# RWKV recursion in a two-layer trunk: ties as quarter-array matmuls, keys by token through transposes, key planes by factor, a fixed chain order

## The chip, the cores and the metric

One core of one Trainium2 chip. The metric is the device time of one execution in microseconds (us); the median of three runs is given, and one profiled execution beside it. PE is the matmul engine (TensorE), PEld its weight loads, DVE VectorE, ACT ScalarE, POOL GpSimd, SP the engine that issues DMAs.

## The reference

A decoder trunk of two layers on x of 1 x 512 x 1024, all in float32: a SwiGLU half, attention, a SwiGLU half; then a SwiGLU half, RWKV-7 time mixing, a SwiGLU half. The change lies in the time mixing alone, 16 heads of 64, whose core is a recursion over the tokens:

```python
def rwkv7_step(state, inp):
    r_t, w_t, k_t, v_t, a_t, b_t = inp
    sa = jnp.einsum('bhvk,bhk->bhv', state, a_t)
    state = (state * w_t[:, :, None, :] + sa[..., None] * b_t[:, :, None, :]
             + v_t[..., None] * k_t[:, :, None, :])
    return state, jnp.einsum('bhvk,bhk->bhv', state, r_t)
...
    seqs = (tm(r_h), tm(w_h), tm(k_h), tm(v_h), tm(-kk), tm(kk * a_h))
    _, y = lax.scan(rwkv7_step, jnp.zeros((B, H, N, N), f32), seqs)
```

## The kernel before

The recursion is done in 8 chunks c of 64 tokens (C = 64, NC = 8), for two groups sg of eight heads. A group is four pairs j (m = 4 sg + j), the two heads of a pair on partitions 0 to 63 and 64 to 127. Within a chunk the tokens are tied to each other through a triangular system; between chunks a state of 64 x 64 per head is handed on.

- rw_prep (L1211, per pair) makes the planes of a pair. From the projected k and the gates it forms the scaled queries ar (plane 0 for the a factor, plane 1 for r), the decay at each chunk's end pend, and the scaled keys bk: k x pi and a x pi (a holds the b factor by then), interleaved by head, tokens side by side. DVE writes the one that belongs to a head's own half (L1263), POOL the other (L1264). Matmuls of 64 x 64 (L1271, 16 per pair) tie keys to queries, DVE masks them into u (L1272), and SP writes u as 32 x 32 tiles to DRAM (L1285, four per pair). rw_prep_all runs the four pairs of a group step by step.
- rw_inverse (L1307) loads the tiles back (L1315), DVE eliminates in 62 small operations (L1324, L1328), ACT transposes (L1329), four small loads and matmuls (L1356, L1363) complete the 64 x 64 inverses.
- rw_prep2 (L1288) forms the r plane on POOL (L1296) and per-head sums (L1297 DVE, L1300 PE).
- rw_ties (L1367), per chunk: POOL makes a diagonal dp of pend (L1379); 8 matmuls (L1384) tie both scaled keys to both queries into two banks, one by head, with 64 rows of the array for each; DVE masks them into am (L1386); 4 matmuls (L1389) with bk against dp give the keys by token, scaled; ACT copies them to bs (L1390); SP fetches v (L1395).
- rw_recur (L1398), per chunk: the right side from v and state (L1417, L1421), an ACT copy (L1427), the solve with the inverse (L1431), ACT copies (L1433), the state update (L1438 on PE, L1441 POOL, L1442 or L1444 DVE), the ties of the next chunk, the output y (L1449, L1453), four ACT copies of y (L1457).
- rw_post and rw_out (L1461, L1498) normalise y, transpose v back (L1480) and project with wo. L1052 and L1021 are the gate's expansion and per-head sums of the same part; L286 to L288 are the three products of a split-float32 matmul.

Nothing here is a table of numbers: a planner in the tile framework sets each engine's order at build time from its own model of times (TileContext with schedule_with_timeline_sim), subject to data dependences and to `self.after(x, y)`, which only demands that x come later than y in the order. "bank(name, n)" takes one of n PSUM banks of that name in turn. The callers, in the order of the text:

```python
        self.rw_prep_all(0)
...
        self.rw_inverse(0, mid)
        self.rw_prep_all(1)
...
        self.rw_prep2(1)
        self.rw_inverse(1, None)
        self.rw_recur(0)
...
        self.rw_recur(1)
        z = self.rw_post(0)
```

An f32 matmul shows in the trace as two instructions (two loads, two matmuls), in the listings of the order as one row.

## Time and profile before

| | us |
|---|---|
| median of 3 runs | 2183.55 (2183.04 to 2183.78) |
| the profiled execution | 2181.74 |
| its span, first to last instruction | 2179.5 |
| mean granted PE clock | 0.984 |

The profile counts an engine as busy while an instruction of it runs. In tables by stretch, PEclk is the granted clock as a share of 2.4 GHz. In brackets behind a row stands the idle time ahead of it and what ended it. The time mixing spans about 1380 to 1800 us; the rest are the attention and the SwiGLU halves.

### The profile page before, as it was taken

What the parts mean: (1) busy time and instruction counts of PE and PEld (TensorE: products, weight loads), DVE (VectorE), ACT (ScalarE), POOL (GpSimd) and SP (SyncE); (2) the same over time, 40 slices, a digit from 0 to 9 for tenths busy, and PEclk for the clock granted to TensorE, in tenths of its full rate; (3) what the DMA queues carried; (4) which work ended last, traced back from release to release, by engine and by line L of the source; (5) the groups of instructions that cost most, each with busy time, mean ns of one, the idle gap of its engine ahead of it and who ended that gap; (6) DMA issues with size and microseconds to landing.
All of it is one profiled execution on the core that took longest, in us unless ns stands there. A gap on an engine that the chain in (4) does not pass through costs nothing.

```text
span 2179.5 us, 28535 instructions
## 1 busy us (share of the span) xinstructions
PE 2136.5 (98%) x11431; PEld 1729.6 (79%) x11431; DVE 1185.3 (54%) x1595; ACT 775.9 (36%) x1196; POOL 219.8 (10%) x224
## 2 busy tenths in 40 slices
PE   8999999999999999999999999999989999999999
PEld 6888887867988888888888888767658768888887
DVE  5444445377478554447545445668576555444443
ACT  4222224345326332335333333462513334222222
POOL 2000002010011000002000000153462101000000
PEclk9999999999999999999999999999979999999999
DMA  5232323411018555555555655457633143232331
GB/s 177 78 116 78 111 92 108 121 49 54 20 58 268 190 184 184 170 192 188 169 191 156 184 172 162 171 164 223 178 112 91 51 158 97 77 116 81 108 102 58
DMA packets 264092, 286.56 MB, mean 131 GB/s; under 512 B 45139, under 2 KB 221419, under 8 KB 263960
## 3 DMA queue, kind: packets, MB, share of 16 engines
q1 hardware_dynamic: 261848, 282.65, 41.7%
q10 hardware_dynamic: 2112, 2.10, 0.3%
q8 instruction: 89, 1.46, 0.3%
q14 instruction: 43, 0.35, 0.0%
HBM read 229.85 MB, written 56.68 MB: 131 GB/s over the span
## 4 chain that ended last, share of the span: by engine, by line
PE 90%; DVE 6%; DMA 1%; ACT 1%; issue 1%; SPq 0%; POOL 0%; DVEq 0%; ACTq 0%; POOLq 0%
PE b L286 22%; PE b L287 22%; PE b L288 22%; PE am L286 3%; PE am L287 3%; PE am L288 3%; DVE const L1324 1%; PE ra L1384 1%; PE rm L286 1%; PE rm L287 1%; PE rm L288 1%; PE wo L287 1%; PE wo L286 1%; PE wo L288 1%; DVE heads L1263 1%; PE rq L1021 1%
## 5 line engine op out<-in xcount | busy, mean ns | idle before, releaser
L287 PE MATMUL b<-xg,parts 128*128 128x512 f32 x1408 | 548.5, 390 | 0.0
L286 PE MATMUL b<-xg,parts 128*128 128x512 f32 x1408 | 547.1, 391 | 1.2 <-ACT xg L385 0.8
L288 PE MATMUL b<-xg,parts 128*128 128x512 f32 x1408 | 547.7, 390 | 0.0
L258 DVE TENSOR_TENSOR parts<-const,parts 128x1024 fp32r<-128x1024 f32 (+2 forms) x320 | 362.1, 1138 | 292.2 <-ACT parts L257 291.6
L257 ACT CAST parts<-const 128x1024 fp32r<-128x1024 f32 (+2 forms) x320 | 312.2, 976 | 476.9 <-PE b L287 398.4
L286 PEld LDWEIGHTS b<-xg,parts 128*128 128x128 f32 x1408 | 264.6, 188 | 57.7 <-ACT xg L385 1.2
L287 PEld LDWEIGHTS b<-xg,parts 128*128 128x128 f32 x1408 | 264.7, 188 | 56.2 <-issue 1.0
L288 PEld LDWEIGHTS b<-xg,parts 128*128 128x128 f32 x1408 | 264.4, 188 | 55.0 <-issue 0.2
L288 PE MATMUL b<-act,parts 128*128 128x512 f32 x704 | 273.3, 389 | 0.0
L287 PE MATMUL b<-act,parts 128*128 128x512 f32 x704 | 273.2, 389 | 0.0
L286 PE MATMUL b<-act,parts 128*128 128x512 f32 x704 | 272.4, 390 | 0.0
L373 POOL TENSOR_TENSOR ssum<-ssum,sq 128x512 f32<-128x512 f32 x42 | 66.0, 1571 | 1211.3 <-ACT sq L372 544.8
L288 PEld LDWEIGHTS b<-act,parts 128*128 128x128 f32 x704 | 132.2, 188 | 27.5
L286 PEld LDWEIGHTS b<-act,parts 128*128 128x128 f32 x704 | 132.2, 188 | 27.3
L287 PEld LDWEIGHTS b<-act,parts 128*128 128x128 f32 x704 | 132.2, 188 | 27.2
L498 DVE SCALAR_TENSOR_TENSOR const<-b,const 128x512 f32<-128x512 f32 x128 | 87.3, 687 | 113.2 <-PE b L288 113.2
L291 ACT CAST act<-u 128x512 fp32r<-128x512 f32 x88 | 54.6, 622 | 246.5 <-DVE u L484 246.5
L483 DVE TENSOR_TENSOR u<-b,rstd 128x512 f32<-128x512 f32 x88 | 60.5, 690 | 148.0 <-PE b L288 147.9
L92 ACT ACTIVATE g<-g 128x512 f32<-128x512 f32 x88 | 55.2, 630 | 190.3 <-DVE g L478 190.3
L478 DVE TENSOR_TENSOR g<-b,rstd 128x512 f32<-128x512 f32 x88 | 60.2, 688 | 95.5 <-PE b L288 95.3
L292 DVE TENSOR_TENSOR act<-u,act 128x512 fp32r<-128x512 f32 x88 | 60.5, 689 | 36.5 <-ACT act L291 36.2
L484 DVE TENSOR_TENSOR u<-u,g 128x512 f32<-128x512 f32 x88 | 60.5, 691 | 2.7
(329 smaller groups left out, 2692.3 us busy)
## 6 DMA issues: line engine op xcount, KB each, us to landing
const<-in_ffn_w_gate_dram SPq DMA_DIRECT2D x88, 512.0 KB
const<-in_ffn_w_up_dram SPq DMA_DIRECT2D x88, 512.0 KB
parts<-pparts SPq DMA_DIRECT2D x68, 512.0 KB
parts<-parts SPq DMA_DIRECT2D x68, 512.0 KB
const<-in_ffn_w_down_dram SPq DMA_DIRECT2D x64, 512.0 KB
const<-in_ffn_w_down_dram SPq DMA_DIRECT2D x48, 256.0 KB
const<-in_attn_w_in_dram SPq DMA_DIRECT2D x24, 512.0 KB
lora<-pparts SPq DMA_DIRECT2D x8, 576.0 KB
```

What stands on the lines that cost most here:

```text
L92: ins = nc.scalar.activation(out, in_, func, **kw)
L257: self.nc.scalar.copy(hi[:r, :n], raw[:, :n])
L258: self.lo_engine.tensor_tensor(out=lo[:r, :n], in0=raw[:, :n], in1=hi[:r, :n].bitcast(F32), op=ALU.subtract)
L286: self.after(mm(out, lhs[0], rhs[0], start=start, stop=False), self.gate)
L287: mm(out, lhs[0], rhs[1], start=False, stop=False)
L288: self.last_mm = mm(out, lhs[1], rhs[0], start=False, stop=stop)
L292: self.nc.vector.tensor_tensor(out=lo, in0=t, in1=hi.bitcast(F32), op=ALU.subtract)
L373: nc.gpsimd.tensor_tensor(out=ssum, in0=ssum, in1=sq, op=ALU.add)
L478: nc.vector.tensor_tensor(out=g, in0=ps[i], in1=rstd, op=ALU.mult)
L483: nc.vector.tensor_tensor(out=u, in0=ps[2 + i], in1=rstd, op=ALU.mult)
L484: nc.vector.tensor_tensor(out=u, in0=u, in1=gs[i], op=ALU.mult)
L498: nc.vector.scalar_tensor_tensor(out=self.x[c], in0=ps, scalar=0.5, in1=self.x[c], op0=ALU.mult, op1=ALU.add)
```

## The change

In rw_prep the interleaved bk goes; two planes take its place, kp (from k) and bp (from a), each written by one DVE product over all 128 partitions (L1260 and L1261 after). POOL has no product there any more. In rw_ties POOL multiplies the keys of the chunk by pend into dp (same size as the diagonal was). The ties become 16 matmuls of 64 rows by 64 columns, 128 moving columns each, in the order pair, factor, head, each chained behind the one before; the banks "ra" are three instead of two. The keys by token come from four PE transposes of dp and three ACT copies. In rw_recur the next chunk's L1422 (after) must come behind the solve of the chunk before, L1456 behind the state update, and y is copied by one ACT instruction. Line numbers after the change are a few lower in rw_prep (L1271 is L1268, L1272 is L1269, L1386 is L1388) and a few higher in rw_recur (L1421 is L1427, L1431 is L1437, L1438 is L1445).

```diff
--- before.py
+++ after.py
@@ -1256,23 +1256,20 @@
         )
         pend = self.pend[:, sg, j, :, None]
         nc.gpsimd.tensor_copy(pend, ar[:, 1, :, C - 1 : C])
-
-        bk = heads[:, 2:4].rearrange("p e c t -> p (e c t)").rearrange("p (c e t) -> p c e t", c=NC, e=2)
-        for hh in range(2):
-            hs = slice(hh * 64, (hh + 1) * 64)
-            nc.vector.tensor_tensor(out=bk[hs, :, hh, :], in0=ch(k)[hs], in1=ch(pi)[hs], op=ALU.mult)
-            nc.gpsimd.tensor_tensor(out=bk[hs, :, 1 - hh, :], in0=ch(a)[hs], in1=ch(pi)[hs], op=ALU.mult)
+        kp, bp = heads[:, 2], heads[:, 3]
+        nc.vector.tensor_tensor(out=kp, in0=ch(k), in1=ch(pi), op=ALU.mult)
+        nc.vector.tensor_tensor(out=bp, in0=ch(a), in1=ch(pi), op=ALU.mult)
         yield
 
         ps = self.bank("rq", 3).rearrange("p (c t) -> p c t", c=NC)
         for c in range(NC):
             for hh in range(2):
                 own, oth = self.halves[hh]
-                mm(ps[oth, c, :], bk[own, c, 1 - hh, :], ar[own, 0, c, :], start=True, stop=True)
+                mm(ps[oth, c, :], bp[own, c, :], ar[own, 0, c, :], start=True, stop=True)
         nc.vector.tensor_tensor(
             out=u, in0=ps, in1=self.cmask[:, 0:1, :].to_broadcast([P, NC, C]), op=ALU.mult
         )
-        rw[m] = dict(ar=ar, bk=bk, u=u)
+        rw[m] = dict(ar=ar, kb=(kp, bp), u=u)
 
         if j == 0:
             rw["lin", sg] = self.dram.tile([P, 1024], F32, name=f"lin{sg}")
@@ -1373,21 +1370,29 @@
         bn = bs[:, 0].rearrange("p (j h d) -> p j h d", j=4, h=2)
         sv = bs[:, 1].rearrange("p (h j d) -> p h j d", h=2, j=4)
 
-        dp = self.diag[:, c % 2].rearrange("p (j d) -> p j d", j=4)
-        pend = self.pend[:, sg, :, c, None].to_broadcast([P, 4, P])
-        ident = self.ident[:, None, :].to_broadcast([P, 4, P])
-        self.after(nc.gpsimd.tensor_tensor(out=dp, in0=ident, in1=pend, op=ALU.mult), self.go)
-        ps = [self.bank("ra", 2).rearrange("p (j n) -> p j n", j=4) for _ in range(2)]
+        kb = rw["heads", sg][:, :16].rearrange("p (j i) c t -> p j i c t", i=4)[:, :, 2:, c, :]
+        dp = self.diag[:, c % 2].rearrange("p (j e t) -> p j e t", j=4, e=2)
+        pend = self.pend[:, sg, :, c, None, None].to_broadcast([P, 4, 2, C])
+        self.after(nc.gpsimd.tensor_tensor(out=dp, in0=kb, in1=pend, op=ALU.mult), self.go)
+        ps, ins = [self.bank("ra", 3).rearrange("p (j n) -> p j n", j=4) for _ in range(2)], None
         for j in range(4):
             pp = rw[4 * sg + j]
-            for h, (own, _) in enumerate(self.halves):
-                mm(ps[h][:, j, :], pp["bk"][own, c], pp["ar"][own, :, c, :], start=True, stop=True)
+
+            for e in range(2):
+                for h in range(2):
+                    own, to = self.halves[h][0], self.halves[h][e]
+
+                    prev, ins = ins, mm(ps[h][to, j, :], pp["kb"][e][own, c, :], pp["ar"][own, :, c, :], start=True, stop=True)
+                    self.after(ins, prev)
         for h in range(2):
             nc.vector.tensor_tensor(out=am[:, h], in0=ps[h], in1=mask, op=ALU.mult)
-        ps = self.bank("ra", 2)
+        ps = self.bank("ra", 3)
         for j in range(4):
-            mm(ps[:, j * P : (j + 1) * P], rw[4 * sg + j]["bk"][:, c], dp[:, j, :], start=True, stop=True)
-        nc.scalar.copy(bs[:, 0], ps)
+            nc.tensor.transpose(ps[:, j * P : (j + 1) * P], self.diag[:, c % 2, j * P : (j + 1) * P], self.ident)
+        ps = ps.rearrange("p (j h d) -> p j h d", j=4, h=2)
+        nc.scalar.copy(bn[:, :, 0], ps[:, :, 0])
+        for own, oth in self.halves:
+            nc.scalar.copy(bn[own, :, 1], ps[oth, :, 1])
 
         b, r0 = c // 2, (c % 2) * 64
         src = rw["vcd"][b][r0 : r0 + 64, :].rearrange("p (m h d) -> p m h d", h=2, d=C)
@@ -1406,7 +1411,7 @@
         self.am = self.t("am", [2, 2, 4, 2 * C]) if sg else self.shaped(self.raw_all[:, :2048], [2, 2, 4, 2 * C])
         self.bs = self.t("bs", [2, 2, S]) if sg else self.shaped(self.call[:, N_CONST + 4 * S : N_CONST + 8 * S], [2, 2, S])
         self.go = self.rr[0, 3] if sg else self.mid
-        st = None
+        st = solved = None
         am, bn, sv = self.rw_ties(sg, 0)
         for c in range(NC):
             b1 = self.bank("rr", 3).rearrange("p (q j v) -> p q j v", q=2, j=4)
@@ -1414,7 +1419,8 @@
             ps = b1[:, 0]
             for j in range(4):
                 for h, (own, oth) in enumerate(self.halves):
-                    mm(ps[oth, j, :], am[own, h, j, :C], sv[own, h, j, :], start=j == 0, stop=c == 0 and j == 3)
+                    ins = mm(ps[oth, j, :], am[own, h, j, :C], sv[own, h, j, :], start=j == 0, stop=c == 0 and j == 3)
+                    self.after(ins, solved)
             if c:
                 for j in range(4):
                     for h, (own, oth) in enumerate(self.halves):
@@ -1428,14 +1434,15 @@
             ps = b2[:, 0]
             for j in range(4):
                 for h, (own, oth) in enumerate(self.halves):
-                    mm(ps[oth, j, :], pairs[j]["u"][oth, c, :], rhs[oth, j, :], start=True, stop=True)
+                    solved = mm(ps[oth, j, :], pairs[j]["u"][oth, c, :], rhs[oth, j, :], start=True, stop=True)
+            moved = solved
             for h, (own, oth) in enumerate(self.halves):
                 nc.scalar.copy(sv[oth, h], ps[oth])
             if c < NC - 1:
                 ps = b2[:, 1]
                 for j in range(4):
                     for h, (own, _) in enumerate(self.halves):
-                        mm(ps[own, j, :], bn[:, j, h, :], sv[:, h, j, :], start=True, stop=True)
+                        moved = mm(ps[own, j, :], bn[:, j, h, :], sv[:, h, j, :], start=True, stop=True)
                 if c:
                     pend = self.pend[:, sg, :, c, None].to_broadcast([P, 4, C])
                     nc.gpsimd.tensor_tensor(out=part, in0=st, in1=pend, op=ALU.mult)
@@ -1446,15 +1453,15 @@
             py = b1[:, 1]
             for j in range(4):
                 for h, (own, oth) in enumerate(self.halves):
-                    mm(py[own, j, :], sv[:, h, j, :], am[:, h, j, C:], start=j == 0, stop=c == 0 and j == 3)
+                    ins = mm(py[own, j, :], sv[:, h, j, :], am[:, h, j, C:], start=j == 0, stop=c == 0 and j == 3)
+                    self.after(ins, moved)
             if c:
                 for j in range(4):
                     for h, (own, oth) in enumerate(self.halves):
                         self.rr[sg, NC] = mm(
                             py[own, j, :], st[own, j, :], pairs[j]["ar"][own, 1, c, :], start=False, stop=j == 3
                         )
-            for j in range(4):
-                nc.scalar.copy(pairs[j]["ar"][:, 0, c, :], py[:, j, :])
+            nc.scalar.copy(self.rw["heads", sg][:, 0:16:4, c, :], py)
             if c < NC - 1:
                 st, am, bn, sv = new, am2, bn2, sv2
 
```

PE in the first prep, at the third and fourth pair's products of keys and queries. Before:

```order
L288 MATMUL rm<-parts,xm 128x512
L1271 MATMUL rq<-heads 64x64 x16
L1021 MATMUL rq<-norms,const 8x512
L1271 MATMUL rq<-heads 64x64 x15
L1021 MATMUL rq<-norms,const 8x512 x2
```

After, at the same place:

```order
L287 MATMUL rm<-parts,xm 128x512
L1268 MATMUL rq<-heads 64x64 x32
L1021 MATMUL rq<-norms,const 8x512 x3
L288 MATMUL rm<-parts,xm 128x512
L286 MATMUL rm<-parts,xm 128x512
```

Before, 17 more matmuls of L1271 stand ahead, with five projection products (L286 to L288) between them and the first row shown, so that the two pairs come in three pieces; after, both pairs are one block of 32 (L1268), with the three L1021 behind it.

DVE in the second prep, from the last two pairs' products to the last mask. Before:

```order
L1263 TENSOR_TENSOR heads<-kr,heads 64x8x64 x2
L1272 TENSOR_TENSOR heads<-rq,const 128x512
L1263 TENSOR_TENSOR heads<-kr,heads 64x8x64 x2
L1386 TENSOR_TENSOR const<-ra,const 128x512
L1444 COPY recur<-rr 128x256
L1386 TENSOR_TENSOR const<-ra,const 128x512
L1297 SCALAR_TENSOR_TENSOR kr<-kr,const,kback 128x512 x3
L1386 TENSOR_TENSOR const<-ra,const 128x512
L1297 SCALAR_TENSOR_TENSOR kr<-kr,const,kback 128x512
L1272 TENSOR_TENSOR heads<-rq,const 128x512
L1386 TENSOR_TENSOR const<-ra,const 128x512
L1272 TENSOR_TENSOR heads<-rq,const 128x512 x2
```

After:

```order
L1260 TENSOR_TENSOR heads<-kr,heads 128x512
L1261 TENSOR_TENSOR heads<-const,heads 128x512
L1260 TENSOR_TENSOR heads<-kr,heads 128x512
L1451 COPY recur<-rr 128x256
L1260 TENSOR_TENSOR heads<-kr,heads 128x512
L1269 TENSOR_TENSOR heads<-rq,const 128x512
L1388 TENSOR_TENSOR const<-ra,const 128x512 x2
L1269 TENSOR_TENSOR heads<-rq,const 128x512
L1294 SCALAR_TENSOR_TENSOR kr<-kr,const,kback 128x512 x2
L1269 TENSOR_TENSOR heads<-rq,const 128x512
L1294 SCALAR_TENSOR_TENSOR kr<-kr,const,kback 128x512 x2
```

The half-height products L1263 are full-height L1260 and L1261; the masks L1269 (L1272 before) stand closer behind them, two of three ahead of L1294 (L1297 before).

PE in one chunk of the second recursion. Before:

```order
L1421 MATMUL rr<-recur,heads 64x64 x8
L1389 MATMUL ra<-const,heads 128x128 x4
L1384 MATMUL ra<-heads 128x128 x4
L1431 MATMUL rr<-recur,heads 64x64 x8
L1417 MATMUL rr<-bs,am 64x64 x8
L1384 MATMUL ra<-heads 128x128 x4
L1449 MATMUL rr<-am,bs 64x64
L1438 MATMUL rr<-bs 64x64 x8
L1449 MATMUL rr<-am,bs 64x64 x7
L1453 MATMUL rr<-heads,recur 64x64 x8
```

After:

```order
L1427 MATMUL rr<-recur,heads 64x64 x8
L1385 MATMUL ra<-heads 64x128 x16
L1391 MATMUL ra<-const 128x128 x4
L1052 MATMUL rq<-hids 128x512
L1437 MATMUL rr<-recur,heads 64x64 x8
L1422 MATMUL rr<-bs,am 64x64 x8
L1052 MATMUL rq<-hids 128x512 x3
L1445 MATMUL rr<-bs 64x64 x8
L1456 MATMUL rr<-am,bs 64x64 x8
```

The ties L1384, half ahead of the solve L1431 and half behind L1417, are one block L1385 ahead of the transposes and the solve L1437; L1456 and L1461 stand behind the state update L1445.

## Rows read from the trace of the kernel before

**Rows 1.** The page: busy time by engine, the chain by engine
```profile
PE 2136.5 (98%) x11431; PEld 1729.6 (79%) x11431; DVE 1185.3 (54%) x1595; ACT 775.9 (36%) x1196; POOL 219.8 (10%) x224
PE 90%; DVE 6%; DMA 1%; ACT 1%; issue 1%; SPq 0%; POOL 0%; DVEq 0%; ACTq 0%; POOLq 0%
```

**Rows 2.** Busy us by 20 us stretch: PE, PEld, DVE, ACT, POOL; PEclk, DMA, GB/s
```profile
1460.00:1480.00 20.00, 16.01 (x160) 11.43 (x159) 18.08 (x20) 0.72 (x1) 14.15 (x10) 0.83 0.45 153
1600.00:1620.00 20.00, 17.75 (x166) 15.91 (x166) 15.89 (x17) 3.60 (x7) 17.88 (x14) 0.50 0.19 46
1620.00:1640.00 20.00, 16.93 (x177) 9.86 (x178) 10.88 (x28) 3.48 (x10) 1.50 (x4) 0.84 0.21 47
1640.00:1660.00 20.00, 19.12 (x352) 17.25 (x344) 19.07 (x43) 6.07 (x23) 5.09 (x6) 0.96 0.16 36
1700.00:1720.00 20.00, 20.00 (x230) 15.36 (x229) 12.13 (x19) 7.46 (x18) 3.13 (x3) 1.00 0.06 14
1720.00:1740.00 20.00, 20.00 (x232) 15.85 (x233) 7.16 (x11) 5.34 (x16) 3.20 (x3) 0.91 0.31 94
```

**Rows 3.** The timeline of PE in the first prep: start, us, what, idle before
```profile
1461.25 1.15 PE L1271 MATMUL rq<-heads 64*64 64x64 f32 x32
1471.84 0.44 PE L1271 MATMUL rq<-heads 64*64 64x64 f32 x2 [3.99 <-DVE heads L1254]
1475.07 2.29 PE L1271 MATMUL rq<-heads 64*64 64x64 f32 x32
```

**Rows 4.** By line (ns min/median/max, first and last start), then the timeline
```profile
L1254 DVE TENSOR_SCALAR heads<-heads x8: 168/1232/1261, 1453.9 to 1599.5; 128x8 f32<-128x8 f32 x8
L1263 DVE TENSOR_TENSOR heads<-kr,heads x16: 674/1550/1768, 1455.1 to 1604.6; 64x512 f32<-64x512 f32 x16
...
1597.20 3.45 POOL L1264 TENSOR_TENSOR heads<-pa,heads 64x512 f32<-64x512 f32 x2
1600.73 6.70 POOL L1264 TENSOR_TENSOR heads<-const,heads 64x512 f32<-64x512 f32 x4
...
1621.41 0.69 DVE L1272 TENSOR_TENSOR heads<-rq,const 128x512 f32<-128x512 f32 x1 [1.01 <-PE rq L1271]
```

**Rows 5.** The timeline from tile writes to elimination's end, SP and DVE
```profile
1617.55 7.88 SPq L1285 DMA_DIRECT2D lin<-heads  x12
1626.68 0.34 SPq L1315 DMA_DIRECT2D const<-lin  x1
...
1630.36 0.19 DVE L1324 TENSOR_TENSOR const<-const 128x31 f32<-128x31 f32 x1 [4.73 <-DMA const<-lin]
1663.74 0.19 DVE L1328 TENSOR_TENSOR const<-const 128x31 f32<-128x31 f32 x1
```

**Rows 6.** The timeline, PE in the second recursion; last, a line's durations
```profile
1684.34 0.63 PE L1431 MATMUL rr<-recur,heads 64*64 64x64 f32 x16
1692.80 0.68 PE L1421 MATMUL rr<-recur,heads 64*64 64x64 f32 x16
1693.41 1.16 PE L1389 MATMUL ra<-const,heads 128*128 128x128 f32 x8
1694.50 1.16 PE L1384 MATMUL ra<-heads 64*128 64x128 f32 x8
1695.59 0.51 PE L1431 MATMUL rr<-recur,heads 64*64 64x64 f32 x10
1696.05 0.51 PE L1417 MATMUL rr<-bs,am 64*64 64x64 f32 x11
1696.49 1.16 PE L1384 MATMUL ra<-heads 64*128 64x128 f32 x8
1716.03 0.66 PE L1480 MATMUL rq<-const,heads 128*128 128x128 f32 x4
1763.85 1.88 PE L1021 MATMUL rq<-heads,const 128*8 128x512 f32 x4
...
L1390 ACT COPY bs<-ra x8: 585/585/585, 1674.9 to 1745.4; 128x512 f32<-128x512 f32 x8
```

## The prediction

> **What bounds the kernel now.** I read the page's busy line and chain first. PE is busy 98% of a span of 2179.5 us and 90% of the chain that ended last is PE [rows 1], so an edit pays where it takes work from PE or where it ends a stretch in which PE runs thin. The table by 20 us stretches shows where that is: almost everywhere PE is busy 19 to 20 us of 20 at clock 1.00; the exceptions that this change touches lie between 1460 and 1480 and between 1600 and 1640 [rows 2]. Those are the key preparations (prep) of the first and of the second eight heads. There DVE and POOL are the busy ones (DVE 18.08, POOL 14.15 of 20 at 1460), PE waits and the granted clock falls to half: 0.50 means 1.2 of 2.4 GHz. From 1640 to 1660 DVE is again the bound (19.07 of 20), in the triangular inverse of the second eight heads, under which the first recursion runs. From 1680 to 1764, the second recursion beside the first group's output projection, PE is dense (20.00 of 20 at 1700 and 1720). The profiled execution took 2181.74 us, its span 2179.5; the median of the runs is 2183.55, 1.8 more. I sum against 2181.74 and add 1.8.
>
> **Part 1: prep of the first eight heads.** Per head pair, two DVE and two POOL products of 64 partitions become two DVE products of 128; DVE's count stays. What goes is POOL's share and what it does to DVE: L1254, eight columns, costs DVE 168 ns at best but 1232 in the median, L1263 674 and 1550 [rows 4]; in prep the long ones lie beside POOL products, the short ones don't. In the first prep PE waits 3.99 us for the keys of the third pair; the row names DVE L1254, but L1254 had ended before, and what was still running are POOL's products, the matmul's own operand. Behind that wait PE runs slow: a group of 32 takes 2.29 us where an earlier one takes 1.15, and the stretch has clock 0.83 [rows 3, 2]. Matmuls of about 5.4 us there cost some 2.7 more than at full clock, so 6.7 us can be won at most. Against it stands the new order: PE asks for two pairs at once, 32 matmuls together (excerpt on PE above), so it waits for DVE's second of each two; DVE still has to do eight products of some 0.68 us and the L1251s before them, and I work out about 3.3 us of wait. I take -3.3; the ends are 0 and -6.7.
>
> **Part 2: prep and inverse of the second eight heads.** Eight POOL products go; the last six take 3.45 + 6.70 us [rows 4], about 1.68 each, so 13.4 in all. Until 1606 they keep DVE's products and L1254s at the long price: some eight DVE operations there pay about 1 us too much each. The new order on DVE (excerpt above) has the masks L1269 and the ties' masks closer behind the products. The last mask now ends at 1622.1 [rows 4]; with products and L1254s at the short price and half the ties out of PE's way (PE is at clock 0.50 here, so it has them at half speed) I put it at about 1608. The rest is a chain: SP issues the sixteen tile writes until 1625.43, the load follows at 1626.68, DVE starts the inverse at 1630.36, ends its elimination at 1663.93 [rows 5], and the second recursion's first solve starts at 1684.34 [rows 6]. So the inverse could start 14 us earlier. It won't end 14 earlier, for DVE then has two more mask products of 0.64 and about 1.5 us of waiting inside its 33.6. I take -11.5 at its end and pass that on to 1684.34, since the 20.4 us between are copies, writes, loads and the inverse's own matmuls, which the change leaves. The ends: -4 if the load is held by something else for most of it, -15 if all of it arrives. In 1640 to 1664 cheaper ties bring nothing: DVE sets the pace there, and I count nothing for the first recursion.
>
> **Part 3: the second recursion, 1684.34 to 1763.85** [rows 6]. Each chunk's ties were two groups of 8 instructions (4 matmuls of 64 rows by 128 columns, two instructions each): the groups start 1.09 us before the next work, so 136 ns an instruction, 2.18 us a chunk. The two heads use different rows of the array and yet gain nothing on the 136 ns of the 128 by 128 group of L1389. Now it is 32 instructions of 64 by 64, moving 128. No such row exists. Nearest: L1421, 64 by 64 moving 64, alternates between two quarters and takes 0.61 us for 16, 38 ns each; where L1431 and L1417 run into each other, with all four quarters in play, 32 take 0.90 (1695.59 to 1696.49), 28 ns each. If a fixed part a and a shared part b make these, a + b/2 = 38 and a + b/4 = 28, so b = 40 and a = 18. Moving twice as much, four quarters in turn: 18 + 2 x 40/4 = 38 ns, 1.22 us a chunk. The ends: 136/4 = 34 ns (1.09 us) and 2 x 28 = 56 ns (1.79 us). I take 1.22, between them and nearer to the lower, because the row with four quarters is mostly fixed part: 0.96 us saved.
>
> The keys by token: four f32 matmuls with a scaled diagonal, 8 instructions in 1.09 us, become four transposes; L1480 shows four, the next group 0.41 us later [rows 6]; 0.65 to 0.68 saved, I take 0.65. So 1.61 a chunk. Of the seven chunks whose ties come after the first, six lie in this dense stretch: 9.7 us. Against it: the evacuation of the keys becomes three ACT copies, of 256 or fewer elements, for one of 0.585 [rows 6], on the engine that must also deliver the solve's right side and result; all sixteen ties now stand in one block ahead of the solve, where half stood behind it (excerpt on the chunk above); and the fixed order adds waits: L1422 only behind the previous solve, L1456 behind the state update. Behind these waits stand, on PE, the output projection's matmuls that the order put there. What hides ACT's copies today is PE's tie block; it gets 1.6 us shorter. I charge 0.4 us a chunk, 2.4; the ends are 0 and two more copies of 0.585 lying bare in each, 7.0. Part 3: -7.3, ends 6 x (1.09 + 0.65) = 10.4 with no waits, and +0.8 (56 ns ties save 0.39, transposes 0.65, six of them 6.2, against 7.0).
>
> The y copy, one instead of four, is 0.56 us of ACT in either case and off the path. The scaled keys on POOL are as large as the diagonals were; nothing. What is after 1764 (second group's output, last FFN) is unchanged.
>
> **Sum:** -3.3 - 11.5 - 7.3 = -22.1; 2181.74 - 22.1 + 1.8 = 2161.4, I say **2161.5**.
>
> A rule speaks against the transposes: the Trainium skill, "TensorE: Matmul & The Clock Gate", Part 4, says that a transpose doesn't count as PE being busy for the clock in the way a matmul does. The trace partly disagrees: the stretch from 1700 to 1720 has two groups of L1480 transposes and clock 1.00; the one behind, with no PE idle either, has 0.91 [rows 2, 6].
>
> **The rivals.**
> (a) Only two quarters run at once. By the two-quarter row, and by the half-array row where two row halves gained nothing: 136/2 = 68 ns, 2.18 us, as now. Part 3 is then 6 x 0.65 - 2.4 = -1.5; time 2167. Chance 0.12.
> (b) The inverse's start isn't passed on. For it: the inverse competes on DVE with the first recursion's masks, POOL's clearing of its buffer must be early, and 1620 to 1640 has PE at 16.93 with waits of its own. Part 2 gives 0 to -2: 2171. Chance 0.13.
> (c) The clock. Stretches of about 3.4 us at half clock (what 0.91 in 1720 to 1740 comes to) appear in each of the eight chunks: half of 3.4 lost, 1.7 x 8 = 13.6 back; time 2175. That is what the page's rule would do here. Chance 0.07.
> (d) Slower: the quarters run one behind the other. Each depends in order on the one before by the fixed chain, and 32 small instructions bring 32 weight loads. At 136 ns each they take 4.35 us a chunk, 2.17 more than now; part 3 is 6 x (2.17 - 0.65) + 2.4 = +11.5, the first recursion becomes bound by PE and takes 6 of part 2 away: -3.3 - 5.5 + 11.5, 2186. At 1.5 times that, 204 ns, with loads left bare: another 6 x 2.2 + 8 = 21, 2207. It decides from about 130 ns an instruction. Against it: 28 ns in the four-quarter rows. I name 2190 for it. Chance 0.11.
>
> **How the numbers follow.** Forecast 0.57, mostly within 2150 to 2173: all lower ends at once (6.7, 15, 10.4) give 2151.4, all upper ones (0, 4, -0.8) 2180.3, and it is unlikely that all fall on one side. A measurement can tell about 0.2% here, 4.4 us, so "same" is 2179.2 to 2187.9. Faster by more: forecast 0.57, (a) 0.12, (b) 0.11, (c) 0.05 = 0.85, less 0.02 for slips inside the forecast, 0.83. Same: 0.02 of (b), 0.02 of (c), 0.03 of (d) and those 0.02 = 0.09. Slower: 0.08 of (d). The range of 2148 to 2178: below lies 0.05 (all lower ends and something I haven't costed), above it 0.13, most of it (d).
>
> **What would show it.** Part 1: no wait above 3.5 us at the first prep's L1268 and no group of it above 1.5 us. Part 2: first inverse operation (L1321) near 1613 (1616 less part 1's 3), first solve of the second recursion near 1670, no POOL product beside L1260. Part 3: a chunk's sixteen ties within 1.1 to 1.8 us, transposes in about 0.4, 72 us from that solve to the end of the projection. It is wrong if a tie block takes 2 us or more, if DVE's inverse starts after 1622, or if PE shows new waits on ACT's key copies of more than 1 us a chunk.

## The result, and the profile after

The median is 2154.97 us of 4 runs (2153.18 to 2156.56), against 2183.3 of the kernel before (2178.98 to 2183.78, 4 runs): ratio 0.9878, 95% interval 0.9866 to 0.9889, 28 us or 1.2% faster. The profiled execution took 2156.56, the slowest of the four; its span is 2154.9, 24.6 less than before. The stages below are told from the two profiled executions, so they add up to 24.6.

The page after, busy time and chain, to be held against [rows 1]:

```profile
span 2154.9 us, 28881 instructions
PE 2104.1 (98%) x11623; PEld 1697.2 (79%) x11623; DVE 1165.4 (54%) x1595; ACT 781.2 (36%) x1180; POOL 192.7 (9%) x208
...
PE 91%; DVE 6%; DMA 1%; issue 1%; ACT 1%; POOL 0%; SPq 0%; DVEq 0%; ACTq 0%; POOLq 0%
```

PE is as much the bound as it was; it has 32 us less of busy time. POOL lost 27 us, the sixteen products that it no longer makes. The four stretches of the time mixing between marks that both kernels have: from the first tie matmul to the load that starts the second elimination, to the elimination's end, to the first solve of the second recursion, to the per-head sums behind it. In the kernel after (columns as in [rows 2]):

```profile
1542.40:1601.90 59.50, 54.52 (x620) 37.02 (x619) 44.93 (x58) 27.62 (x49) 35.44 (x30) 0.94 0.56 160
1601.90:1640.70 38.80, 27.67 (x598) 21.63 (x597) 32.92 (x80) 12.84 (x34) 8.38 (x9) 0.91 0.14 36
1640.70:1667.04 26.34, 22.30 (x605) 18.60 (x598) 7.25 (x12) 11.46 (x25) 3.77 (x4) 0.87 0.45 118
1667.04:1738.20 71.16, 67.91 (x1053) 49.77 (x1049) 31.57 (x50) 29.75 (x70) 8.81 (x10) 0.98 0.42 124
```

The same four stretches of the kernel before:

```profile
1548.80:1626.70 77.90, 69.12 (x628) 51.19 (x629) 56.08 (x60) 28.21 (x51) 48.80 (x39) 0.80 0.42 128
1626.70:1663.90 37.20, 33.24 (x553) 28.33 (x553) 31.73 (x77) 10.25 (x35) 7.42 (x8) 0.91 0.15 37
1663.90:1684.34 20.44, 20.15 (x522) 17.89 (x519) 7.47 (x13) 9.38 (x23) 3.76 (x4) 1.00 0.60 151
1684.34:1763.85 79.51, 78.30 (x978) 60.47 (x975) 32.56 (x50) 28.34 (x85) 9.76 (x10) 0.98 0.38 111
```

The first solve of the second recursion in the kernel after is this row:

```profile
1667.04 0.58 PE L1437 MATMUL rr<-recur,heads 64*64 64x64 f32 x14
```

The L1437 ahead of it, at 1662.80, is the last chunk of the first recursion: it runs side by side with the second group's first right side (L1422, from 1663.10), which the second recursion's first solve needs. From 1667.04 on PE has 128 solve instructions, eight chunks of 16, as many as before from 1684.34 on.

The first tie matmul comes 6.4 us earlier (part 1). Then the first stretch shrinks by 18.4, and the one row tells how: PE busy 54.5 for 69.1 us, granted clock 0.94 for 0.80, PE idle 5.0 for 8.8. The elimination takes 1.6 longer, the stretch behind it 5.9, the second recursion 8.4 less; what follows the sums is 1.1 longer. -6.4 - 18.4 + 1.6 + 5.9 - 8.4 + 1.1 = -24.6.

PE in the first prep, for [rows 3] (start, us, what, idle before):

```profile
1460.98 1.15 PE L1268 MATMUL rq<-heads 64*64 64x64 f32 x32
1463.22 1.15 PE L1268 MATMUL rq<-heads 64*64 64x64 f32 x32 [1.09 <-DVE heads L1261]
1467.46 2.15 PE L1268 MATMUL rq<-heads 64*64 64x64 f32 x64
```

The wait of 3.99 is 1.09, no group runs at half clock (64 instructions now take 2.15, the 32 of before took 2.29), and the stretch's clock is 1.00 where it was 0.83.

DVE's eight-column operation by line (ns min/median/max, first and last start), for [rows 4]:

```profile
L1254 DVE TENSOR_SCALAR heads<-heads x8: 159/161/2120, 1453.6 to 1589.7; 128x8 f32<-128x8 f32 x8
```

SP's timeline after, the last tile writes and the load, for [rows 5]:

```profile
1597.77 2.42 SPq L1282 DMA_DIRECT2D lin<-heads  x5
1601.88 0.34 SPq L1312 DMA_DIRECT2D const<-lin  x1
```

DVE's timeline after, the last mask of the second prep, the first and the last operation of the second elimination:

```profile
1597.69 0.68 DVE L1269 TENSOR_TENSOR heads<-rq,const 128x512 f32<-128x512 f32 x1
...
1605.85 0.19 DVE L1321 TENSOR_TENSOR const<-const 128x31 f32<-128x31 f32 x1 [3.69 <-DMA const<-lin]
...
1640.49 0.18 DVE L1325 TENSOR_TENSOR const<-const 128x31 f32<-128x31 f32 x1
```

L1254's median falls from 1232 to 161 ns. The last mask ends at 1598.4 for 1622.1, the elimination starts at 1605.85 for 1630.36 and ends at 1640.7 for 1663.9.

PE's timeline in the second recursion, its longest wait, then one chunk's ties, transposes and the next work, for [rows 6]:

```profile
1670.71 0.69 PE L1445 MATMUL rr<-bs 128*64 128x64 f32 x16 [1.97 <-ACT bs L1440]
...
1700.18 1.04 PE L1385 MATMUL ra<-heads 64*64 64x128 f32 x28
1701.15 0.66 PE L1391 MATMUL ra<-const 128*128 128x128 f32 x4
1701.74 0.50 PE L1052 MATMUL rq<-hids 8*128 8x512 f32 x1
```

ACT's timeline ahead of that wait:

```profile
1667.72 2.19 ACT L1020 ACTIVATE heads<-heads 128x512 f32<-128x512 f32 x4
1669.92 0.75 ACT L1440 COPY bs<-rr 64x256 f32<-64x256 f32 x2
```

28 instructions from 1700.18 to 1701.15 are 35 ns each, where a half-array instruction took 136; four transposes take 0.59 to the next work. L1445 waits 1.97 us for the solve's copies L1440, since four activations of the first group's output (L1020, 2.19 us) stand ahead of them on ACT.

### The profile page after: what moved, and what is told of

It reads as the page before. It is cut to its first block, busy times and chain, and to the rows that moved or that the text cites. A ratio compares the mean times of both kernels' runs of the same rounds, so it can differ in the third digit from the quotient of the medians.

```text
span 2154.9 us, 28881 instructions
## 1 busy us (share of the span) xinstructions
PE 2104.1 (98%) x11623; PEld 1697.2 (79%) x11623; DVE 1165.4 (54%) x1595; ACT 781.2 (36%) x1180; POOL 192.7 (9%) x208
## 4 chain that ended last, share of the span: by engine, by line
PE 91%; DVE 6%; DMA 1%; issue 1%; ACT 1%; POOL 0%; SPq 0%; DVEq 0%; ACTq 0%; POOLq 0%
PE b L286 22%; PE b L288 22%; PE b L287 22%; PE am L286 3%; PE am L287 3%; PE am L288 3%; PE rm L286 1%; PE rm L287 1%; PE rm L288 1%; DVE const L1321 1%; PE wo L286 1%; PE rq L1021 1%; DVE inv L1325 1%; PE wo L287 1%; PE wo L288 1%
## 5 line engine op out<-in xcount | busy, mean ns | idle before, releaser
L286 PE MATMUL b<-xg,parts 128*128 128x512 f32 x1408 | 547.0, 391 | 1.2 <-ACT xg L385 0.7
L288 PE MATMUL b<-xg,parts 128*128 128x512 f32 x1408 | 547.7, 390 | 0.0
L286 PEld LDWEIGHTS b<-xg,parts 128*128 128x128 f32 x1408 | 264.5, 188 | 57.2 <-ACT xg L385 1.1
L288 PEld LDWEIGHTS b<-xg,parts 128*128 128x128 f32 x1408 | 264.4, 188 | 55.2 <-DVE parts L258 0.3
L288 PE MATMUL b<-act,parts 128*128 128x512 f32 x704 | 273.3, 389 | 0.0
L286 PE MATMUL b<-act,parts 128*128 128x512 f32 x704 | 272.4, 390 | 0.0
L288 PEld LDWEIGHTS b<-act,parts 128*128 128x128 f32 x704 | 132.1, 188 | 27.3
L286 PEld LDWEIGHTS b<-act,parts 128*128 128x128 f32 x704 | 132.1, 188 | 27.2
```

What stands on the lines that cost most here:

```text
L286: self.after(mm(out, lhs[0], rhs[0], start=start, stop=False), self.gate)
L288: self.last_mm = mm(out, lhs[1], rhs[0], start=False, stop=stop)
```

## Experiments

Four kernels put one part alone on the kernel before (a1 to a4), two put two parts on it (c1, c4), six change one thing in the changed kernel (b1 to b4, c2, c3). The table gives the ratio to the kernel before, the median, and from the profiled execution (us): the load that starts the second elimination (SP), the start of the elimination's last operation, the first solve of the second recursion, the start of its last output matmul from the ties (L1449, L1456 after), the span, and the mean granted clock.

| kernel | ratio (95%) | median | load | elimination | first solve | last output | span | clock |
|---|---|---|---|---|---|---|---|---|
| before | | 2183.3 | 1626.7 | 1663.7 | 1684.3 | 1757.4 | 2179.5 | 0.984 |
| changed | 0.9878 (0.9866 to 0.9889) | 2155.0 | 1601.9 | 1640.5 | 1667.0 | 1731.7 | 2154.9 | 0.989 |
| a1, products on DVE | 0.9964 (0.9952 to 0.9976) | 2172.7 | 1614.5 | 1652.2 | 1677.6 | 1751.2 | 2173.3 | 0.990 |
| a2, quarter ties | 1.0001 (0.9985 to 1.0016) | 2180.3 | 1623.2 | 1656.9 | 1686.9 | 1752.8 | 2175.6 | 0.986 |
| a3, transposes | 1.0037 (1.0025 to 1.0050) | 2189.6 | 1627.4 | 1668.0 | 1688.9 | 1769.7 | 2191.9 | 0.980 |
| a4, chain order | 1.0020 (1.0008 to 1.0032) | 2185.3 | 1623.8 | 1661.4 | 1686.5 | 1759.2 | 2184.0 | 0.985 |
| c1, a1 and a2 | 1.0022 (1.0012 to 1.0033) | 2187.1 | 1617.7 | 1652.6 | 1686.9 | 1750.2 | 2184.2 | 0.980 |
| c4, a1 and a3 | 0.9956 (0.9939 to 0.9972) | 2171.3 | 1613.3 | 1653.8 | 1675.2 | 1747.2 | 2169.5 | 0.989 |
| b1, changed, other tie order | 0.9904 (0.9886 to 0.9921) | 2161.7 | 1601.9 | 1638.8 | 1671.7 | 1737.2 | 2159.3 | 0.988 |
| b2, changed, no chain order | 0.9863 (0.9848 to 0.9878) | 2153.3 | 1601.4 | 1640.7 | 1664.3 | 1729.4 | 2152.0 | 0.990 |
| b3, changed, diagonal keys | 0.9884 (0.9864 to 0.9904) | 2156.9 | 1604.7 | 1641.8 | 1669.2 | 1737.6 | 2160.8 | 0.990 |
| b4, changed, POOL products | 0.9949 (0.9931 to 0.9967) | 2171.3 | 1609.5 | 1646.0 | 1679.4 | 1746.5 | 2169.3 | 0.985 |
| c2, changed, two banks | 0.9892 (0.9865 to 0.9919) | 2157.6 | 1601.9 | 1637.5 | 1671.1 | 1731.2 | 2153.0 | 0.986 |
| c3, changed, mask ahead | 0.9887 (0.9873 to 0.9902) | 2157.3 | 1602.1 | 1644.6 | 1664.5 | 1734.5 | 2156.2 | 0.988 |

The runs of the kernel before on the chips of the three sets had medians of 2180.2 (a), 2182.3 (b) and 2181.8 (c); across sets the ratios are the ones to compare. The marks of a kernel come from one execution. The planner orders every kernel anew, so one edit moves rows that it doesn't touch.

**a1, products on DVE.**

```diff
-            nc.gpsimd.tensor_tensor(out=bk[hs, :, 1 - hh, :], in0=ch(a)[hs], in1=ch(pi)[hs], op=ALU.mult)
+            nc.vector.tensor_tensor(out=bk[hs, :, 1 - hh, :], in0=ch(a)[hs], in1=ch(pi)[hs], op=ALU.mult)
```

> The kernel before, with POOL's two half-height key products per pair (L1264) given to DVE, which then has four instead of two; layout, ties, keys by token and order of the chain as before. Theory (the gain of the whole change comes first of all from POOL no longer running beside DVE in the two preps): although DVE gets 16 products of 0.68 us more, 5.4 us a group, L1254 and L1251 fall to 0.17 and 0.67 us behind the last POOL work, the wait of 4.0 us and the half clock in the first prep go, the elimination of the second group starts 8 to 14 us earlier than at 1630.4, and the time falls by 8 to 15 us, to 2169 to 2176. Rival 1 (POOL's products only cost because DVE had to wait for them, and one engine for all is no faster): DVE's extra work eats the gain, time within 4 us of 2183. Rival 2 (the gain comes from the cheaper ties at half clock in 1595 to 1640): within 4 us of 2183 too, with the elimination's start within 3 us of 1630.

The load came 12.2 us earlier, the elimination's end 11.5, though DVE had eight more products a group; the time fell by 0.36%, 8 us, the small end of what the theory said. Both rivals fall. But of 11.5 us at the elimination's end only 6.8 arrive at the first solve of the second recursion and 6.2 at the last output. The first solve comes 0.7 us behind the first recursion's last output (1676.9): the elimination is not the only thing that stands ahead of it.

**a2, quarter ties.**

```diff
+        ins = None
...
-            for h, (own, _) in enumerate(self.halves):
-                mm(ps[h][:, j, :], pp["bk"][own, c], pp["ar"][own, :, c, :], start=True, stop=True)
+            for e in range(2):
+                for h in range(2):
+                    own, to = self.halves[h][0], self.halves[h][e]
+                    q = h ^ e
+                    prev, ins = ins, mm(ps[h][to, j, :], pp["bk"][own, c, q, :], pp["ar"][own, :, c, :], start=True, stop=True)
+                    self.after(ins, prev)
```

> The kernel before, with only the ties changed: 16 matmuls of 64 by 64 per chunk in the order pair, factor, head, each chained behind the one before; banks, products, keys by token and chain order as before. Theory: a chunk's 32 instructions take 1.1 us at full clock for 2.18, which is worth 6 x 1.0 = 6 us in the second recursion, less some waiting, and some 3 us more where the half clock made ties cost double in 1595 to 1640, so the time is 2174 to 2179. Rival 1 (PE's order decides, the freed time is lost in waits for ACT and DVE): within 4 us of 2183. Rival 2 (ties are the main part of the 28 us): 2165 or less, elimination starting 10 us or more earlier.

No difference that can be told, so rival 1. The profiled execution shows where it went: PE's waits from 1590 to 1770 (for whom: us, times, longest):

```profile
PE rq L1271 <- DVE recur L1449: 9.5, 1, 9.5
PE rr L1422 <- DVE const L1391: 7.8, 4, 3.6
PE rr L1454 <- ACT const L1438: 4.5, 1, 4.5
```

PE now gets to the products of keys and queries (L1271) before DVE and POOL have their keys, and stands there 9.5 us in one piece: in the second prep DVE and POOL are the bound, and what PE saves there is given back as waiting. In the second recursion the theory's 6 us do come: from its first solve to its last output it takes 65.9 us for 73.1. They are lost ahead of it: the elimination ends 6.8 earlier, yet the first solve comes 2.5 later (1686.9), right behind the first recursion, which these waits have made late (last output 1686.2 for 1683.7).

**a3, transposes.**

```diff
+        kb = rw["heads", sg][:, :16].rearrange("p (j i) c t -> p j (i c t)", i=4)[:, :, 2 * S :]
+        kb = kb.rearrange("p j (c n) -> p j c n", c=NC)[:, :, c, :]
...
-        ident = self.ident[:, None, :].to_broadcast([P, 4, P])
-        self.after(nc.gpsimd.tensor_tensor(out=dp, in0=ident, in1=pend, op=ALU.mult), self.go)
+        self.after(nc.gpsimd.tensor_tensor(out=dp, in0=kb, in1=pend, op=ALU.mult), self.go)
...
-            mm(ps[:, j * P : (j + 1) * P], rw[4 * sg + j]["bk"][:, c], dp[:, j, :], start=True, stop=True)
+            nc.tensor.transpose(ps[:, j * P : (j + 1) * P], self.diag[:, c % 2, j * P : (j + 1) * P], self.ident)
```

> The kernel before, with only the keys by token changed: POOL scales the keys by the chunk's decay, four PE transposes turn them, one ACT copy as before (the layout stays interleaved, so that one copy does). Theory: 8 instructions in 1.09 us become 4 in 0.4 to 0.45; six chunks in the dense stretch, 4 us; time 2178 to 2181. Rival 1 (transposes leave the clock at half in each chunk): mean clock below 0.98 and the time 2190 or more. Rival 2 (the keys are never late, nothing is won): within 2 us of 2183.

0.37% slower, 8 us, near rival 1 and against the theory. The stretches of 5 us behind its elimination (1668.0):

```profile
1665.00:1670.00 5.00, 5.00 (x88) 4.32 (x88) 4.00 (x11) 3.32 (x5) 2.03 (x2) 1.00 0.26 88
1670.00:1675.00 5.00, 2.51 (x48) 2.06 (x48) 1.46 (x3) 1.65 (x7) 0.07 (x1) 0.93 0.63 184
1675.00:1680.00 5.00, 4.67 (x99) 4.10 (x100) 0.68 (x1) 1.33 (x4) 0.00 (x0) 0.50 1.02 199
1680.00:1685.00 5.00, 5.00 (x137) 4.44 (x138) 0.00 (x0) 0.48 (x2) 0.00 (x0) 0.50 0.57 142
1685.00:1690.00 5.00, 5.00 (x56) 4.09 (x52) 1.36 (x2) 4.15 (x11) 1.05 (x1) 0.50 0.97 266
1690.00:1695.00 5.00, 5.00 (x87) 4.40 (x86) 0.68 (x1) 0.58 (x1) 0.00 (x0) 0.50 0.16 41
1695.00:1700.00 5.00, 5.00 (x8) 0.69 (x6) 0.00 (x0) 0.00 (x0) 0.00 (x0) 0.68 0.00 0
1700.00:1705.00 5.00, 4.32 (x65) 2.98 (x64) 3.00 (x5) 3.46 (x10) 1.14 (x1) 1.00 0.00 0
```

Two rows of its PE timeline, the gap and the work during which the clock rose:

```profile
1675.33 0.28 PE L1356 MATMUL rq<-const,heads 32*32 32x32 f32 x2 [2.82 <-DMA const<-tout]
...
1694.82 5.26 PE L1021 MATMUL rq<-heads,const 128*8 128x512 f32 x8
```

PE runs dry at 1672 to 1675, waiting 2.82 us for the eliminated tiles' way through DRAM; then the clock is 0.50, and stays so for 20 us though PE is shown busy 5.00 of 5.00. It rises in the stretch with the eight matmuls L1021. From 1675 to 1697 half the speed is some 11 us, which is the loss. Whether the transposes did it or the gap, this run can't say; b3 and c4 can.

**a4, chain order.** On the kernel before, the lines of the change with `solved` and `moved`:

```diff
+                    ins = mm(ps[oth, j, :], am[own, h, j, :C], sv[own, h, j, :], start=j == 0, stop=c == 0 and j == 3)
+                    self.after(ins, solved)
...
+                    ins = mm(py[own, j, :], sv[:, h, j, :], am[:, h, j, C:], start=j == 0, stop=c == 0 and j == 3)
+                    self.after(ins, moved)
```

> The kernel before, with only the order of the chain fixed: L1417 behind the solve of the chunk before, L1449 behind the state update. Theory: no work goes, so nothing or a small loss by waits; 2181 to 2187. Rival (the order is what makes the whole change work, since L1449 no longer stands among L1438 ahead of the state): 2177 or less.

0.2% slower, as the theory had it. The order alone gains nothing.

**b1, other order of the ties.**

```diff
-            for e in range(2):
-                for h in range(2):
+            for h in range(2):
+                for e in range(2):
```

> The changed kernel with one thing else: the sixteen ties of a chunk go pair, head, factor, so two neighbours share the rows of one head and write to different columns of the result, where the change alternates between the heads. Theory (alternating is what lets quarters run together): a chunk's 32 instructions take 1.6 to 2.2 us for 1.1, some 6 to 10 us over the recursion, time 2160 to 2166. Rival (any order of four quarters overlaps as well, so that the order within a chunk is of no weight): 1.1 us a chunk, time within 3 us of 2155.

The time, 2161.7, is what the theory said, and the theory is wrong. One chunk's ties in this kernel, and the next work:

```profile
1704.66 1.04 PE L1385 MATMUL ra<-heads 64*64 64x128 f32 x29
1705.63 0.33 PE L1391 MATMUL ra<-const 128*128 128x128 f32 x1
```

29 instructions in 0.97 us, 33 ns each, no more than the 35 with the heads alternating. That is the rival's mechanism: the order of the four quarters is of no weight. The 6 us come from the new plan: the elimination ends 1.7 us earlier than in the changed kernel, yet the second recursion's first solve comes 4.7 later (1671.7), and from there to the last output it takes 65.5 us for 64.7. So 0.8 us of the loss lie where these ties stand dense; the rest lies ahead of it. I have no run that holds everything else in place.

**b2, no chain order.** In the changed kernel:

```diff
-                    self.after(ins, solved)
...
-                    self.after(ins, moved)
```

> The changed kernel without the fixed order of the chain (no demand on L1422 after the solve of the chunk before nor on L1456 after the state update). Theory (alone on the kernel before, the order cost 4 us; it takes no work away): 2150 to 2158. Rival (with cheap ties the planner would put output and next chunk's matmuls ahead of the state update and so lengthen the chain; the order is worth several us here): 2160 or more.

2153.3, as the theory said; the intervals of the two kernels overlap, so that it beats the changed kernel isn't shown, only that the order is worth nothing here.

**b3, diagonal keys.**

```diff
-        kp, bp = heads[:, 2], heads[:, 3]
+        bk = heads[:, 2:4].rearrange("p e c t -> p (e c t)").rearrange("p (c n) -> p c n", c=NC)
+        kp, bp = bk[:, :, :C], bk[:, :, C:]
...
-            nc.tensor.transpose(ps[:, j * P : (j + 1) * P], self.diag[:, c % 2, j * P : (j + 1) * P], self.ident)
+            mm(ps[:, j * P : (j + 1) * P], rw[4 * sg + j]["bk"][:, c], dp[:, j, :], start=True, stop=True)
```

> The changed kernel with the keys by token made again by four f32 matmuls with a diagonal on POOL, the key products written with a chunk's two factors side by side so that one load takes them; quarter ties, products on DVE, three ACT copies and chain order stay. Theory 1 (transposes save 0.65 us of PE a chunk): 4 to 7 us slower than the changed kernel, 2159 to 2162. Theory 2 (what the transposes alone on the kernel before showed, 8 us slower, is their own doing, through the clock): the kernel gets faster without them, 2145 to 2151. Theory 3 (that loss was a gap of PE ahead of the completion of the inverse and not the transposes): as theory 1, and the clock in the 40 us behind the elimination's end is no better than now (0.87).

2156.9, 2 us above the changed kernel within intervals that overlap: between theories 1 and 2, and without the gain that theory 2 asks for. The clock from 1640 to 1680 is 0.91 for the changed kernel's 0.87, a little better than theory 3 had it. In the second recursion the diagonal keys cost what was expected of them: 68.4 us from first solve to last output for 64.7, though this profiled execution (2162.5) is the slowest of its four. So the transposes cost nothing here and give at most a few us. c4 says the same.

**c4, products on DVE and transposes.** The diffs of a1 and a3 together.

> All four half-height key products on DVE, and the keys by token through transposes; ties, banks and chain as before. Against the kernel with the products alone (2173). Theory 1 (transposes save 0.65 us of PE a chunk and lost 8 us alone by where the gap behind the elimination fell): 2166 to 2172. Theory 2 (transposes themselves keep the clock low): 2178 or more, and the clock behind the elimination's end under 0.9 for 40 us.

2171.3, 1.4 us below a1 with intervals that overlap, and a clock of 0.96 and 1.00 in the 40 us stretches from 1640 and 1680. Beside a1 the transposes lose nothing, so a3's 8 us go with the gap of its plan and not with the transposes by themselves. Theory 2 falls.

**b4, POOL products.**

```diff
-        nc.vector.tensor_tensor(out=bp, in0=ch(a), in1=ch(pi), op=ALU.mult)
+        nc.gpsimd.tensor_tensor(out=bp, in0=ch(a), in1=ch(pi), op=ALU.mult)
```

> The changed kernel with one of the two key products of a pair (L1261, 128 partitions wide) back on POOL. Theory (POOL's products slow DVE and are themselves late): the elimination of the second group starts 6 to 12 us later than at 1605.9 and the time is 5 to 12 us up, 2160 to 2167. Rival (the gain of the preps comes from the full-width layout and the order it allows, and POOL's half of the products is free): within 3 us of 2155.

The dearest undoing of all: 16 us. The load comes 7.6 us later, and behind the elimination PE runs dry. L1254 by line, at its old price again:

```profile
L1254 DVE TENSOR_SCALAR heads<-heads x8: 163/1228/1262, 1453.7 to 1592.6; 128x8 f32<-128x8 f32 x8
```

Its stretch of 40 us behind the elimination (columns as in [rows 2]):

```profile
1640.00:1680.00 40.00, 27.60 (x689) 23.86 (x692) 13.11 (x31) 12.47 (x28) 4.42 (x5) 0.70 0.33 82
```

PE's longest waits in it from 1450 to 1770 (us, times, longest):

```profile
PE rq L1353 <- DMA const<-tout: 10.8, 2, 10.1
PE ra L1385 <- DVE heads L1269: 7.4, 1, 7.4
```

POOL's eight products cost 5.5 us at the elimination's end; the other 9 to the last output come in the 40 us with clock 0.70 and 12.4 us without work. The tiles were not yet back (10.1 us in one wait, until 1652.22), and PE's order had the inverse's matmuls (L1353) ahead of three chunks of the first recursion. The first of their solves:

```profile
1661.34 0.90 PE L1437 MATMUL rr<-recur,heads 64*64 64x64 f32 x10
```

So PE had work left that stood behind the wait. The rows don't show whether all of it could have run before.

**c1, products on DVE and quarter ties.** The diffs of a1 and a2 together.

> The two single parts together on the kernel before: all four half-height key products on DVE and the ties as quarters, alternating; nothing else. Alone they gave -7.4 and 0 us. Theory (the two need each other: the earlier elimination is passed on only where PE has less to do, and PE's saving only counts once the elimination no longer holds the second recursion): 2158 to 2165, that is 15 to 22 us off, more than the sum. Rival 1 (parts add up): 2171 to 2176. Rival 2 (what matters is the full-width layout and the third bank): as rival 1, and the changed kernel's other parts carry the rest.

Slower than either part, and against every theory. Up to the last output it stands 1.0 us ahead of a1; 11.9 us are lost behind it, in work that neither part touches (stretches of 10 us, columns as in [rows 2]):

```profile
1750.00:1760.00 10.00, 10.00 (x66) 6.62 (x63) 2.20 (x4) 3.23 (x9) 0.00 (x0) 1.00 0.72 217
1760.00:1770.00 10.00, 8.53 (x30) 4.62 (x28) 4.01 (x7) 1.35 (x2) 0.00 (x0) 1.00 0.41 146
1770.00:1780.00 10.00, 8.74 (x24) 5.67 (x24) 5.51 (x9) 2.12 (x4) 0.00 (x0) 0.56 0.17 60
1780.00:1790.00 10.00, 10.00 (x29) 5.99 (x27) 5.31 (x8) 2.10 (x4) 0.00 (x0) 0.59 0.01 3
1790.00:1800.00 10.00, 7.98 (x28) 5.83 (x27) 7.44 (x10) 4.02 (x7) 0.23 (x1) 0.83 0.51 143
1800.00:1810.00 10.00, 10.00 (x46) 8.29 (x45) 3.58 (x5) 3.07 (x5) 3.68 (x3) 1.00 0.38 118
```

PE's longest wait in it behind 1750:

```profile
PE rq L1052 <- ACT hids L291: 2.7, 1, 2.7
```

Its plan leaves PE a gap of 2.7 us in the second group's output, and some 17 us at half clock follow, with PE at the output projection's long matmuls; half of that is 8.5, the gap the rest but a us. Ten runs lie between 2181 and 2191, so it belongs to this kernel's order. The 1.0 us ahead of that hides two larger terms. From first solve to last output the second recursion takes 63.3 us for a1's 73.7, so the ties are worth 10.4 there. The first solve comes 9.3 later than a1's (1686.9 for 1677.6), though the elimination ends within 0.4 us of a1's: between the two PE is idle for 6.7 us and the clock is 0.75, where a1 has 2.4 and 1.00.

**c2, two banks.**

```diff
-        ps = self.bank("ra", 3)
+        ps = self.bank("ra", 2)
```

and the same in the line for the two banks of the ties.

> The changed kernel with two banks for the ties and the keys instead of three. Theory (a chunk needs three of them in a row, with two the next chunk's ties wait for the key copies on ACT): 2 to 5 us slower, 2157 to 2160. Rival (ties are issued so far ahead that the bank is free anyway): within 2 us of 2155.

2157.6 with runs from 2152.9 to 2166.5: inconclusive.

**c3, mask ahead.**

```diff
-        self.rw_inverse(1, None)
         self.rw_recur(0)
+        self.rw_inverse(1, None)
...
+            if sg and i == 1:
+                self.after(step, self.masks[0, 2])
```

> The changed kernel, with the second group's elimination written behind the first recursion and made to let chunk 2's masks of the first recursion go ahead of its second step (order only, no work changes). The wait of 7.2 us on PE near 1606 goes. Theory (the elimination, its tile traffic and the second recursion set the end; the first recursion only has to be done beside them): the wait goes, the elimination ends 1 to 2 us later, time within 3 us of 2155. Rival (the first recursion is late too, since half of PE's time behind the elimination is its chunks at half clock): 2147 to 2151.

The wait of 7.2 us became 4.8, the first recursion ended 9 us earlier (its last output at 1657.4 for 1666.4), the elimination 4.1 later, and the last output came 2.8 later, the time 2 us. The time is the theory's. Its reason isn't shown: with the first recursion out of the way the second one's first solve comes 2.6 earlier (1664.5), as the rival wants, and 19.7 behind the elimination's end, close to the 20.4 of the kernel before. The second recursion then takes 5.3 longer. From first solve to last output in this kernel, and under it in the changed one:

```profile
1664.45:1734.46 70.01, 65.04 (x1053) 48.81 (x1048) 31.36 (x51) 26.15 (x63) 8.80 (x10) 0.94 0.31 92
1667.04:1731.75 64.71, 61.46 (x1012) 44.71 (x1008) 30.88 (x49) 27.18 (x65) 8.81 (x10) 0.97 0.38 114
```

PE is idle 1.7 us longer in it and its clock is lower; why the plan came out so stays open. No version here is shown to beat the changed kernel.

## Why the prediction was right, step by step

The direction and the range held, and the sum of 22.1 stands against 25.2 of the profiled execution and 28.3 of the medians. At the mark that I had named, the second recursion's first solve, parts 1 and 2 gave -14.8 and -17.3 was measured; for part 3, -7.3 and -8.4. But inside part 2 two misses nearly cancel, and that is luck.

**Part 1**: -3.3 said, -6.4 measured, next to the lower end. The wait of 3.3 that I set against the gain was 1.09: for the last two pairs, with POOL silent, DVE ran its L1254s in 0.16 and L1251s in 0.67, so the keys came in time. The half clock went with the wait, and that was the other half of the 6.7. What released the wait of 3.99 I had read wrongly. The row names DVE L1254, and DVE and POOL show that it is right:

```profile
1470.47 1.23 DVE L1254 TENSOR_SCALAR heads<-heads 128x8 f32<-128x8 f32 x1
1466.73 6.68 POOL L1264 TENSOR_TENSOR heads<-const,heads 64x512 f32<-64x512 f32 x4
```

L1254, which writes the query operand, ended at 1471.70, 0.14 us before the matmul. Of POOL's four products the third pair's are the first two, done by 1470.1. So PE waited for DVE at its long price beside POOL and not for POOL's products themselves. The gain stays, since the long price goes with POOL's work: in the kernel after, the wait of 1.09 stands behind the one L1254 that took 2.12, and POOL's L1248 and its clearing of a buffer run beside that one.

**Part 2**: -14 to the elimination's start beyond part 1, -18.1 measured (24.5 less 6.4). The steps that I had, products and L1254s at the short price and fewer ties at half speed, are there. Mis-sized was, as far as I can argue it, what lies in the clock: I priced ties at half speed but left the clock itself at 0.50, while it rose from 0.80 to 0.94 over the stretch; a share of 0.20 of 77.9 us is 15.6 us that half clock took before, 0.06 of 59.5 is 3.6 after, 12 us of difference at most. The experiments split the 18.4 up to the load in another way: a1 brings 12.2 - 4.0 = 8.2 (its first tie is 4.0 earlier), a2 1.1 + 3.5 = 4.6, and the eight half-height products that a1 has more on DVE, 8 x 0.68, are 5.4; together 18.2. That they add up so isn't shown. To the elimination itself I had added 2.5, it was 1.2 (34.8 for 33.6). So its end came 16.8 earlier beyond part 1, where I had 11.5.

**The 20.4 us behind the elimination**, passed on unchanged, became 26.3: PE was idle for 4.0 us there for 0.3 before, and the clock was 0.87 for 1.00. I had counted nothing for the first recursion, but the second one's first solve stands behind it in PE's order. In ten of the fourteen kernels it starts 0.6 or 0.7 us behind the first recursion's last output from the ties (1683.7 and 1684.3 before, 1666.4 and 1667.0 after). In a3, c3 and c4, where that output comes earlier, it starts 19.7 to 21.2 behind the elimination's end, which is what I had assumed for all; c2 fits neither (4.7 and 33.4). So of the 16.8 us only 10.9 were passed on: rival (b) in part, and the reason why my 11.5 fits. b4 shows the same in large, with a wait for the tiles ahead of three chunks.

**Part 3**: -7.3 said, -8.4 measured, and by the steps that I had given. The tie price was right, even below what I took (35 ns for 38), and the transposes gave 0.5 for 0.65. PE's busy time fell by 10.4 where I had 9.7; these prices give 9.4 for six chunks, and the last 1.0 I can't place. PE's idle time rose from 1.2 to 3.3, 2.0 for the 2.4 I charged. The single edits bear the ties out in this stage: 73.1 us from first solve to last output became 65.9 in a2, and a1's 73.7 became 63.3 in c1. The row of ACT names a cause that I didn't have: not the three key copies but the activations of the first group's output ahead of the solve's copies.

**The rivals.** (a) and (d) fall with the 35 ns. (c) is half right: half clock was worth some 11 us in a3 and 8.5 in c1. But the transposes don't bring it. Four chunks' transposes (L1391) lie in this stretch of the changed kernel, and its clock is 1.00:

```profile
1680.00:1720.00 40.00, 39.31 (x689) 29.66 (x689) 26.17 (x41) 19.08 (x45) 7.14 (x8) 1.00 0.25 72
```

The rule of the Trainium skill, "TensorE: Matmul & The Clock Gate", Part 4, by which a transpose doesn't count as PE being busy for the clock in the way a matmul does, would have c4 and the changed kernel at a lower mean clock than a1 and b3; the rows have 0.989 and 0.989 against 0.990 and 0.990. (c)'s eight stretches of 3.4 us at half clock come to 0.006; less than that isn't excluded, for over all their runs b3 has 0.990 to 0.993 and the changed kernel 0.989 to 0.991. (The stretch of the kernel before from 1700 to 1720, at clock 1.00, has three groups of L1480 transposes and not the two that I counted.) What stands ahead of three long stretches at half clock is a gap in PE's work: 2.82 in a3, 2.7 in c1, 10.1 in b4.

**Point by point of what was to show it**: no wait above 3.5 in the first prep (1.09) and no group above 1.5 (64 in 2.15), right; elimination's start near 1613, was 1605.85; first solve near 1670, was 1667.0; ties within 1.1 to 1.8, at the lower end; transposes in about 0.4, 0.59 with what stands behind them; 72 us to the sums, was 71.2.

That the parts add up to the whole is not shown. In the end time the quarter ties alone gave nothing, since what they save in the second recursion was lost ahead of it; the transposes and the order lost 8 and 4 us; undone, transposes and order are worth 2 and -2. Only the move of POOL's products is large in both directions (-8 alone, +16 undone). The quarter ties could not be undone in the changed kernel by themselves, since the planes don't have the layout that a half-array load needs; in b3's layout they could, and that wasn't tried.

## What to carry to other kernels

Where a fast engine shares a stage with a slow helper, look at what the helper does to the price of its neighbour's smallest instructions: an eight-column DVE operation at 1.23 us for 0.16 was the mark of the largest gain here. Cheaper matmuls pay only where PE is the bound: the quarter ties took 7 us off the second recursion in a2 and nothing off the whole, since elsewhere they turned into waits, and a wait of a few us can cost ten more at half clock (a3). An engine that takes its work in a fixed order also hands on an earlier input only if nothing else stands late in that order. So judge an edit by the marks between the stages and the granted clock, not by the end time alone: two of these kernels met or missed a forecast time for reasons that had nothing to do with the edit.

## What the runs showed that I had not expected

- Quarter-array f32 matmuls moving 128 columns issue at 33 to 35 ns each whether neighbours share rows (head by head) or not; half-array ones of two row halves, alternating, took 136 ns, as much as a full 128 by 128.
- After a gap of 2.8 us the clock stayed at 1.2 GHz for some 20 us although PE was shown busy all that time (a3, matmuls of 32 and 64 rows); in c1 it stayed there 17 us with matmuls of 128 rows and 512 columns. After a gap of 2.11 us in the changed kernel half clock was over by about 1655, some 7 us later. What decides between 7 and 20 stays open.
- An order that is only a change of the planner's input moved the end by up to 6 us with every price the same (b1), and by 12 us in a stage that the edit doesn't touch (c1).
